# First block's weight sums of the output stages on VectorE, their stores three units later, last forms stored among the units, half of x reloaded later

## The chip, the cores and the metric

The kernel runs on one core of a Trainium2 chip. The metric is the device time of one execution in microseconds. Before the change three runs gave 2659.91 us (median; 2659.52 to 2662.99).

A core has five engines that run their own queues in order and wait for each other through semaphores: TensorE (PE, matrix products), VectorE (DVE), ScalarE (ACT), GpSimd (POOL) and SyncE (SP), whose queue here issues nearly all DMA transfers. Since each queue is in order, an instruction that waits holds back all that stand behind it on its engine.

## What is computed

Two layers of an encoder over 1024 positions of width 1024, float32. Layer 0 mixes by grouped-query attention, layer 1 by a chunked gMLP; each is followed by a squared-ReLU MLP of width 4096.

```python
for i in range(DEPTH):                                   # DEPTH = 2
    mod = cond @ ada_w[i] + ada_b[i]
    sh1, sc1, g1, sh2, sc2, g2 = jnp.split(mod, N_MOD, axis=-1)
    h = modulate(rmsnorm(x, norm1_g[i]), sh1, sc1)
    if i % N_MIXERS == 0:
        y = gqa_attention(...)
    else:
        y = chunked_gmlp(...)
    x = x + g1[:, None, :] * y
    h = modulate(rmsnorm(x, norm2_g[i]), sh2, sc2)
    x = x + g2[:, None, :] * sq_relu_mlp(h, mlp_w_in[i], mlp_w_out[i])

def chunked_gmlp(h, w_in, b_in, ln_g, ln_b, w_s, b_s, w_out):
    z = jax.nn.gelu(h @ w_in + b_in, approximate=False)
    u, v = jnp.split(z, 2, axis=-1)
    v = layernorm(v, ln_g, ln_b)
    ...                                                  # one 128x128 mix per group
    return (u * v) @ w_out                               # w_out: 3072 x 1024

def sq_relu_mlp(h, w_in, w_out):
    return jnp.square(jax.nn.relu(h @ w_in)) @ w_out     # w_out: 4096 x 1024
```

## The kernel before

Every large product is done by a seven-product scheme on 2 x 2 blocks (Winograd's form of Strassen's), and each product in three matmuls of a split float32: an operand becomes a high part (a cast on ScalarE) and a low part (source minus high part), and hi·hi, hi·lo and lo·hi are added up in PSUM. A *unit* is one product of 128 output rows by 512 positions over four 128-row slices: 12 matmuls of 128x512.

The three **output stages** are the second products of the two MLPs (`wm`) and of the gMLP (`wgo`), all by the class `Out`. It has 4 blocks of the inner dimension for an MLP and 3 for the gMLP. Its units run block by block in the order of the products 1, 2, 6, 7, 4, four units each (the pairs p = 0 to 3 of output rows), 20 units per block. Then, as a tail of 8 units per block, come the products 5 and 3 of all blocks, the last block first. Block 0 is units 0 to 19.

What a unit needs comes from two sides:

- The **weights**: the four blocks 11, 12, 21, 22 are loaded (`load_w`, `load_w2`). Products 6 and 7 need sums of them, made in `prep` (line 1134), three units ahead (`LO`). For product 6: 21 + 22 (line 1138), then that minus 11 (line 1140). For product 7: 12 − 11 (1142), then 22 − 11 (1144). The first sum of each kind is also the weight of product 5 or 3. It is needed only in the tail, and unless the block is the last one it is stored to DRAM by `keep` at once (line 1122) and loaded again by `load_kept` (line 1118). All four run on GpSimd (`G`). After the sum, `prep` casts the high half (line 1152, ScalarE) and subtracts for the low half (line 1153, VectorE), into a buffer of the tag `s`, of which there are five.
- The **forms**: seven combinations of the stage's input per 256 rows, in DRAM (`hidden`, `uv`; named hf). `load_f` loads one (line 1129), eight units ahead of its first unit; `split_f` splits it five units ahead (lines 318 and 319, ScalarE and VectorE).

The forms are written by the stage ahead. Three of a pair's seven are the results themselves (`early`); the other four come from `spread` (lines 1234 to 1237), which returns four store instructions that are put on a list `stores` and taken from it one by one. In the MLP `spread` runs on VectorE, in the gMLP on GpSimd, as do the gMLP's products u·v (`times`, line 1612). What is left on the list when the stage ahead ends is issued at once, before the output stage's first unit: at lines 1351 and 1352 in the MLP. In the gMLP, lines 1659 to 1661 first run the steps that are still due, for the last pair p = 11.

The residual x lies in 16 tiles, x[0] and x[1] for the two halves of the positions. Before the first MLP's and the gMLP's output stage it has been spilled to DRAM (xd), and is loaded again in four groups of four tiles, at the units that the table `XL` gives (line 1259). x[0] is added to from unit 4 on, x[1] only in the tail.

The program text isn't the order on the engines: a scheduler of the framework orders each engine's queue by its own estimate of when things are ready. So both the text and the resulting queues count.

Of the kernel before, what the change touches and what calls it, by code (L numbers as in the profile page):

```python
# [14 lines left out]
ALU = mybir.AluOpType  # L15
# [21 lines left out]
def encoder_kernel(ctx: ExitStack, tc: tile.TileContext, t: dict, out: bass.AP):  # L37
    nc = tc.nc
    V, S, G, T = nc.vector, nc.scalar, nc.gpsimd, nc.tensor
# [7 lines left out]
    def nm(s):  # L47
        uid[0] += 1
        return f"{s}_{uid[0]}"
# [825 lines left out]
    with ExitStack() as es:  # L875
# [132 lines left out]
        for i in range(nu + 2):  # L1008
# [7 lines left out]
            for op in ORDER.split():  # L1016
                f, w, j = op[0], int(op[1]), int(op[2])
# [39 lines left out]
    class Out:  # L1057
# [7 lines left out]
        def __init__(self, wsrc, forms, nblk, gate):  # L1065
            self.wsrc, self.forms, self.nblk, self.gate = wsrc, forms, nblk, gate
            self.n = 28 * nblk
            self.tail = 8 * nblk
            self.w, self.raw, self.f, self.sf, self.acc, self.ps = {}, {}, {}, {}, {}, {}
            last = nblk - 1  # L1070
            self.units = [(b, q, p) for b in range(nblk) for q in "12674" for p in range(4)]
            self.units += [(b, q, p) for q in "53" for b in (last, *range(last)) for p in range(4)]
            self.kept = {(b, q, p): dram.tile([P, 512], F32, name=nm("wf"))
                         for b in range(last) for q in "53" for p in range(4)}
            todo = []

            def at(i, fn, *args):
                todo.append((max(i, -OUT_PRE), len(todo), fn, args))

            for i, (b, q, p) in enumerate(self.units):  # L1080
                if q == "1":
                    at(i - LO - LW, self.load_w, b, "11", p)
                elif q == "2":
                    at(i - LO - (LW if b else LW2), self.load_w, b, "22", p)
                    if p % 2 == 0:
                        at(i - LO - LW, self.load_w2, b, "12", p // 2)
                        at(i - LO - (LW if b else LW2), self.load_w2, b, "21", p // 2)
                elif q in "53" and b < last:
                    at(i - LO - LK, self.load_kept, b, q, p)
            for i in range(0, self.n, 4):  # L1090
                for kt in range(4):
                    at(i + kt - FS - FA, self.load_f, self.units[i][:2] + (kt,))
            for i in range(0, self.n, 4):
                for kt in range(4):
                    at(i + kt - FS, self.split_f, self.units[i][:2] + (kt,))
            for i in range(self.n):
                at(i - LO, self.prep, i)
            self.todo = sorted(todo, key=lambda e: e[:2])

        def ahead(self, i):  # L1100
# [16 lines left out]
            self.w[k] = slot()  # L1117
            nc.sync.dma_start(self.w[k], self.kept[k])

        def keep(self, b, q, p, a):  # L1120
            if b < self.nblk - 1:
                nc.sync.dma_start(self.kept[(b, q, p)], a)
            else:
                self.w[(b, q, p)] = a

        def load_f(self, k):
            b, q, kt = k
# [6 lines left out]
        def prep(self, i):  # L1134
            b, q, p = self.units[i]
            a11, a12, a21, a22 = (self.w.get((b, c, p)) for c in ("11", "12", "21", "22"))
            if q == "6":
                G.tensor_tensor(a21, a21, a22, ALU.add)  # L1138
                self.keep(b, "5", p, self.w.pop((b, "21", p)))
                G.tensor_tensor(a11, a21, a11, ALU.subtract)  # L1140
            elif q == "7":
                G.tensor_tensor(a12, a12, a11, ALU.subtract)
                self.keep(b, "3", p, self.w.pop((b, "12", p)))
                G.tensor_tensor(a11, a22, a11, ALU.subtract)
                del self.w[(b, "11", p)]
            elif q == "4":
                del self.w[(b, "22", p)]
            src = self.w.pop((b, q, p)) if q in "53" else {"1": a11, "2": a12, "6": a11, "4": a22, "7": a11}[q]
            w_ = wide("s", F32R)
            hi, lo = w_[:, :512], w_[:, 512:]  # L1150
            self.sf[i] = hi, lo
            S.copy(hi, src)  # L1152
            V.tensor_tensor(lo, src, f32(hi), ALU.subtract)  # L1153
# [76 lines left out]
    def spread(tiles, dst, spare, eng):  # L1230

        b11, b12, b21, b22 = (tiles[a] for a in ((0, 0), (0, 1), (1, 0), (1, 1)))
        t3 = spare()
        eng.tensor_tensor(t3, b22, b12, ALU.subtract)
        eng.tensor_tensor(b12, b12, b11, ALU.subtract)
        eng.tensor_tensor(b11, b22, b12, ALU.subtract)
        eng.tensor_tensor(b21, b21, b11, ALU.subtract)
        return [lambda: nc.sync.dma_start(dst["7"], t3), lambda: nc.sync.dma_start(dst["5"], b12),
                lambda: nc.sync.dma_start(dst["6"], b11), lambda: nc.sync.dma_start(dst["4"], b21)]
# [16 lines left out]
            x[hf][k] = xslot()  # L1256
            nc.sync.dma_start(x[hf][k], xd[hf][k])

    XL = {-1: (0, 0), 2: (0, 1), 6: (1, 0), 10: (1, 1)}


    class Halves:
# [35 lines left out]
    def mlp(layer, fs, sqs, done, hook):  # L1298
# [4 lines left out]
        stores = []  # L1303
# [18 lines left out]
        n = 16 * 7  # L1322
# [25 lines left out]
            out_.ahead(i - n)  # L1348

        yield from winograd(lambda m: t["wi"][layer, m], 16, f, sink, FIRST, at, lambda: (cut(8), f.update(fs[0])))  # L1350
        while stores:
            stores.pop(0)()

        def at_out(i):
            if i == CUT:
                cut(4)
            if halves and i in XL:
                load_xs(*XL[i])
            if hook and i >= out_.n - out_.tail:
                hook(i - out_.n + out_.tail)  # L1360
# [58 lines left out]
    for ct in range(24):  # L1419
        i, r = divmod(ct, 3)  # L1420
# [129 lines left out]
    def gmlp(f, sqB, done, hook):  # L1550
# [26 lines left out]
        uv = forms_dram(12)  # L1577
        out_ = Out(t["wgo"], uv, 3, mod[:, 1, 2])
        us, vs, mixed, stores = {}, {}, {}, []
# [29 lines left out]

        def times(p, j, hf):  # L1610
            w_ = mixed[(2 * p + j, hf)]
            (G if (j, hf) in TG else V).tensor_tensor(w_, w_, us.pop((2 * p + j, hf)), ALU.mult)
            q = early((j, hf))
            if q:
                stores.append(lambda: nc.sync.dma_start(uv[p][q], w_))

        def spread_uv(p):
            tiles = {(j, hf): mixed.pop((2 * p + j, hf)) for j in range(2) for hf in range(2)}
            while stores:
                stores.pop(0)()  # L1620
            stores.extend(spread(tiles, uv[p], xslot, G))

        order = ((0, 0), (1, 0), (1, 1), (0, 1))
        steps = []
# [4 lines left out]
        for p in range(12):  # L1629
            i = 7 * p  # L1630
# [12 lines left out]
        def upto(i):  # L1643
            while steps and steps[0][0] <= i:
                _, _, fn, args = steps.pop(0)
                fn(*args)

        n = 12 * 7
# [7 lines left out]
        upto(-1)  # L1656
        for _ in winograd(lambda m: t["wu"][m], 12, f, sink, 0, at_u):
            pass
        upto(n + 9)
        while stores:  # L1660
            stores.pop(0)()
        load_xs(*XL[-1])

        def at_out(i):
            if i == CUT:
                cut(4)
            if i in XL:
                load_xs(*XL[i])
            if i >= out_.n - out_.tail:
                hook(i - out_.n + out_.tail)  # L1670
            if i == out_.n - PRE:
                next(mlp1)
# [27 lines left out]
FS = 5  # L1700
FA = 3
LO = 3
TG = ((0, 0), (1, 0), (1, 1), (0, 1))
CUT = 8
MX = 2
LW = 5
# [82 lines left out]
```

## Time and profile before

| | |
|---|---|
| median of 3 runs | 2659.91 us |
| the profiled execution | 2660.25 us |
| its span, first to last instruction | 2658.5 us |
| granted TensorE clock, mean | 0.996 |
| first MLP's output stage | from 962.31 us |
| gMLP's output stage | from 1794.32 us |
| second MLP's output stage | from 2345.95 us |

Times of instructions are microseconds from the start of the span. A row of the timeline gives start, duration, engine, line of the code, operation, output <- inputs, and in brackets how long the engine was idle before it and what ended that. A row of the waits gives who waited, for whom, the total, how many times and the longest. A row of the busy table gives a stretch and, for each engine, busy time and instructions in it, then the granted clock, the share of the DMA engines that was busy, and the rate that they moved. SPq is the SP queue. Names of tiles stand without numbers in the profile (t, s, w, c, x are the pools; out, mix are PSUM tiles).

### The profile page before, as it was taken

The numbers are of one execution on the slowest core, as the hardware profiler recorded it, in microseconds if no ns is written. First come the engines' busy times: TensorE is split into PE (matmuls) and PEld (weight loads), VectorE is DVE, ScalarE is ACT, GpSimd is POOL, SyncE is SP. The second block draws the span as 40 slices with busy tenths as digits, with TensorE's granted clock in tenths as the row PEclk, the third lists the DMA queues.
The fourth block names the chain that finished last, engine by engine and source line by source line (L and its number), as shares of the span: only waits on it lengthen the run. The fifth ranks groups of instructions, "written<-read, shape, count | busy, mean of one in ns | idle before, by whom it ended". The sixth has DMA issues, their size and how long they took to land.

```text
span 2658.5 us, 37214 instructions
## 1 busy us (share of the span) xinstructions
PE 2604.3 (98%) x12788; PEld 2166.5 (81%) x12788; DVE 2188.2 (82%) x3215; ACT 1451.1 (55%) x2616; POOL 819.4 (31%) x591
## 2 busy tenths in 40 slices
PE   7999999999999999999999999998999999999999
PEld 5788999887788878888788888887888788878887
DVE  7868999886999989977886687787978977789974
ACT  4569999945654455446543454444456655455442
POOL 0238776523000034430122054556520000035410
PEclk9999999999999999999999999999999999999999
DMA  8100222243486878644243355567741554478461
GB/s 286 42 33 7 74 88 74 96 128 126 173 289 237 285 268 305 201 135 174 72 135 109 121 181 172 179 210 283 240 135 52 174 174 157 153 278 284 151 209 61
DMA packets 208752, 435.38 MB, mean 164 GB/s; under 512 B 23025, under 2 KB 35441, under 8 KB 208562
## 3 DMA queue, kind: packets, MB, share of 16 engines
q1 hardware_dynamic: 181682, 395.24, 43.8%
q10 hardware_dynamic: 26880, 37.76, 3.9%
q8 instruction: 101, 1.65, 0.3%
q14 instruction: 89, 0.73, 0.1%
HBM read 310.23 MB, written 122.68 MB: 163 GB/s over the span
## 4 chain that ended last, share of the span: by engine, by line
PE 84%; DVE 7%; ACT 2%; DMA 2%; issue 2%; POOL 2%; SPq 0%; DVEq 0%; POOLq 0%; ACTq 0%
PE w L454 10%; PE w L455 10%; PE w L456 10%; PE out L1171 9%; PE out L1172 9%; PE out L1170 9%; PE s L907 4%; PE o L943 4%; PE t L924 4%; PE v L1517 3%; PE v L1518 3%; PE v L1516 3%; PE mix L1601 2%; DVE t L319 1%; PE qkv L559 1%
## 5 line engine op out<-in xcount | busy, mean ns | idle before, releaser
L1171 PE MATMUL out<-t,s 128*128 128x512 f32 x1232 | 481.8, 392 | 9.3 <-DVE t L319 9.2
L1170 PE MATMUL out<-t,s 128*128 128x512 f32 x1232 | 481.8, 392 | 4.0 <-ACT t L318 3.6
L1172 PE MATMUL out<-t,s 128*128 128x512 f32 x1232 | 479.6, 390 | 0.0
L454 PE MATMUL w<-t,s 128*128 128x512 f32 x1168 | 459.8, 395 | 0.0
L455 PE MATMUL w<-t,s 128*128 128x512 f32 x1168 | 454.8, 390 | 1.5 <-DVE t L319 1.5
L456 PE MATMUL w<-t,s 128*128 128x512 f32 x1168 | 454.6, 389 | 0.0
L319 DVE TENSOR_TENSOR t<-t,t 128x512 fp32r<-128x512 f32 x408 | 346.0, 860 | 39.9 <-ACT t L318 29.3
L318 ACT CAST t<-t 128x512 fp32r<-128x512 f32 x408 | 244.4, 616 | 121.9 <-DMA t<-hf 62.2
L1171 PEld LDWEIGHTS out<-t,s 128*128 128x128 f32 x1232 | 232.0, 188 | 63.1 <-DVE t L319 15.0
L1170 PEld LDWEIGHTS out<-t,s 128*128 128x128 f32 x1232 | 231.7, 188 | 55.8 <-ACT t L318 6.9
L1172 PEld LDWEIGHTS out<-t,s 128*128 128x128 f32 x1232 | 232.2, 188 | 47.7
L1138 POOL TENSOR_TENSOR w<-w,t 128x512 f32<-128x512 f32 x32 | 52.2, 1633 | 697.2 <-DMA t<-hf 613.2
L439 ACT CAST s<-w 128x512 fp32r<-128x512 f32 x292 | 174.0, 616 | 164.5 <-PE w L456 109.3
L455 PEld LDWEIGHTS w<-t,s 128*128 128x128 f32 x1168 | 219.4, 188 | 48.2 <-DVE t L319 3.5
L454 PEld LDWEIGHTS w<-t,s 128*128 128x128 f32 x1168 | 219.4, 188 | 48.2 <-issue 3.1
L1152 ACT CAST s<-t 128x512 fp32r<-128x512 f32 x240 | 148.0, 620 | 201.6 <-PE out L1172 143.0
L456 PEld LDWEIGHTS w<-t,s 128*128 128x128 f32 x1168 | 219.3, 188 | 45.4
L440 DVE TENSOR_TENSOR s<-w,s 128x512 fp32r<-128x512 f32 x292 | 220.6, 762 | 42.0 <-ACT s L439 41.4
L1153 DVE TENSOR_TENSOR s<-t,s 128x512 fp32r<-128x512 f32 x240 | 203.8, 850 | 60.7 <-ACT s L1152 59.9
L910 DVE TENSOR_REDUCE mx<-s 128x1 f32<-128x1024 f32 x128 | 156.2, 1220 | 32.8 <-PE s L907 31.5
L933 DVE TENSOR_TENSOR t<-t,t 128x512 fp32r<-128x512 f32 x256 | 164.1, 681 | 15.0 <-ACT t L927 14.2
L943 PE MATMUL o<-t,t 128*128 128x256 f32 x1024 | 162.6, 291 | 0.0
(242 smaller groups left out, 5128.4 us busy)
## 6 DMA issues: line engine op xcount, KB each, us to landing
t<-hf SPq DMA_DIRECT2D x320, 256.0 KB, 3.9
hf<-c SPq DMA_DIRECT2D x156, 256.0 KB, 2.6
w<-in_wi_dram SPq DMA_DIRECT2D x64, 512.0 KB, 4.2
hf<-c ACTq DMA_DIRECT2D x96, 256.0 KB, 2.4
w<-in_ada_dram SPq DMA_DIRECT2D x36, 512.0 KB, 3.6
x<-in_ada_dram SPq DMA_DIRECT2D x64, 256.0 KB, 6.0
t<-in_wm_dram SPq DMA_DIRECT2D x64, 256.0 KB, 5.2
wf<-w SPq DMA_DIRECT2D x64, 256.0 KB, 3.3
```

Source lines behind the costliest of these rows:

```text
L318: S.copy(hi, src)
L319: (eng or V).tensor_tensor(lo, src, f32(hi), ALU.subtract)
L439: S.copy(hi, src)
L440: V.tensor_tensor(lo, src, f32(hi), ALU.subtract)
L454: T.matmul(ps, hi[:, a], th, start=kt == 0, stop=False)
L455: T.matmul(ps, hi[:, a], tl, start=False, stop=False)
L456: T.matmul(ps, lo[:, a], th, start=False, stop=kt == 3)
L943: pin(T.matmul(u.po, vt[st][:, u.g * P : (u.g + 1) * P], src[:, s * 256 : (s + 1) * 256], start=st == 0 and part == 0, stop=st == 7 and pa ...
L1153: V.tensor_tensor(lo, src, f32(hi), ALU.subtract)
L1170: T.matmul(ps, hi[:, a], th, start=begin and kt == 0, stop=False, **g)
L1171: T.matmul(ps, hi[:, a], tl, start=False, stop=False, **g)
L1172: T.matmul(ps, lo[:, a], th, start=False, stop=end and kt == 3, **g)
```

## The change

In block 0 of each output stage the four weight sums of a pair are made on VectorE; the other blocks keep GpSimd. The stores of the first sums (for products 5 and 3) leave `prep` and become steps of their own, `KD` = 3 units after it, in all blocks but the last. What is left of `stores` at the end of the stage ahead is no longer issued in one go but one per unit of the output stage (from unit 3 on in the MLP). In the gMLP the steps due after the stage ahead's last unit, the last pair's products, `spread` and its stores, are taken along with the output stage's units, and for the last pair (p = 11) products and `spread` run on VectorE. The table `TG`, which had all products on GpSimd, goes. The two groups of x[1] are reloaded at units 20 and 30 instead of 6 and 10.

```diff
@@ class Out
             for i in range(self.n):
                 at(i - LO, self.prep, i)
+            for i, (b, q, p) in enumerate(self.units):
+                if q in "67" and b < last:
+                    at(i - LO + KD, self.store_kept, b, "5" if q == "6" else "3", p)
             self.todo = sorted(todo, key=lambda e: e[:2])
...
-        def keep(self, b, q, p, a):
-            if b < self.nblk - 1:
-                nc.sync.dma_start(self.kept[(b, q, p)], a)
-            else:
-                self.w[(b, q, p)] = a
+        def store_kept(self, *k):
+            nc.sync.dma_start(self.kept[k], self.w.pop(k))
...
             a11, a12, a21, a22 = (self.w.get((b, c, p)) for c in ("11", "12", "21", "22"))
+            e = G if b else V
             if q == "6":
-                G.tensor_tensor(a21, a21, a22, ALU.add)
-                self.keep(b, "5", p, self.w.pop((b, "21", p)))
-                G.tensor_tensor(a11, a21, a11, ALU.subtract)
+                e.tensor_tensor(a21, a21, a22, ALU.add)
+                self.w[(b, "5", p)] = self.w.pop((b, "21", p))
+                e.tensor_tensor(a11, a21, a11, ALU.subtract)
             elif q == "7":
-                G.tensor_tensor(a12, a12, a11, ALU.subtract)
-                self.keep(b, "3", p, self.w.pop((b, "12", p)))
-                G.tensor_tensor(a11, a22, a11, ALU.subtract)
+                e.tensor_tensor(a12, a12, a11, ALU.subtract)
+                self.w[(b, "3", p)] = self.w.pop((b, "12", p))
+                e.tensor_tensor(a11, a22, a11, ALU.subtract)
...
-    XL = {-1: (0, 0), 2: (0, 1), 6: (1, 0), 10: (1, 1)}
+    XL = {-1: (0, 0), 2: (0, 1), 20: (1, 0), 30: (1, 1)}
@@ mlp
-        while stores:
-            stores.pop(0)()
 
         def at_out(i):
+            if stores and i > 2:
+                stores.pop(0)()
@@ gmlp
-            (G if (j, hf) in TG else V).tensor_tensor(w_, w_, us.pop((2 * p + j, hf)), ALU.mult)
+            (V if p == 11 else G).tensor_tensor(w_, w_, us.pop((2 * p + j, hf)), ALU.mult)
...
-            stores.extend(spread(tiles, uv[p], xslot, G))
+            stores.extend(spread(tiles, uv[p], xslot, V if p == 11 else G))
...
-        upto(n + 9)
-        while stores:
-            stores.pop(0)()
         load_xs(*XL[-1])
 
         def at_out(i):
+            upto(n + i)
+            if stores:
+                stores.pop(0)()
...
-TG = ((0, 0), (1, 0), (1, 1), (0, 1))
+KD = 3
```

## The prediction, made before the result was known

> **What bounds the kernel now.** I read the page first, for the engine that sets the pace, then the busy table over chosen stretches, then the waits and the instructions in order of time inside them.
>
> ```profile
> span 2658.5 us, 37214 instructions
> PE 2604.3 (98%) x12788; PEld 2166.5 (81%) x12788; DVE 2188.2 (82%) x3215; ACT 1451.1 (55%) x2616; POOL 819.4 (31%) x591
> PE 84%; DVE 7%; ACT 2%; DMA 2%; issue 2%; POOL 2%; SPq 0%; DVEq 0%; POOLq 0%; ACTq 0%
> ```
>
> TensorE (PE) is busy 98% of the span and makes up 84% of the chain that ended last, and the change touches no matmul. So only PE's own holes can be won. The change touches the three output stages; unit 0 of each starts at 962.31, 1794.32 and 2345.95. The next table pairs the first ten units of each stage with an equally long stretch right after.
>
> ```profile
> core 0: us, PE busy (x) PEld busy (x) DVE busy (x) ACT busy (x) POOL busy (x), PEclk, DMA share, GB/s
> 962.30:995.00 32.70, 29.96 (x122) 23.26 (x121) 27.04 (x27) 16.14 (x30) 24.36 (x16) 0.95 0.68 235
> 995.00:1027.70 32.70, 32.70 (x146) 27.08 (x145) 27.36 (x34) 18.75 (x34) 13.61 (x9) 1.00 0.90 331
> 1794.30:1832.00 37.70, 30.75 (x122) 23.33 (x121) 22.66 (x20) 12.98 (x23) 30.92 (x22) 0.91 0.74 257
> 1832.00:1869.70 37.70, 37.70 (x167) 30.94 (x166) 34.23 (x41) 22.04 (x40) 19.12 (x12) 1.00 0.80 289
> 2345.90:2376.30 30.40, 28.08 (x122) 22.33 (x122) 27.08 (x27) 15.68 (x29) 23.09 (x15) 1.00 0.61 214
> 2376.30:2406.70 30.40, 30.37 (x134) 24.84 (x133) 25.31 (x34) 17.70 (x33) 9.45 (x7) 1.00 0.93 344
> ```
>
> Read the matmul counts, not the busy time: a slowed matmul counts as busy. The first stretch does 122 matmuls where the second does 146, 167 and 134. The lost time is 32.70 × (1 − 122/146) = **5.4 us** (first MLP), 37.70 × (1 − 122/167) = **10.2** (gMLP) and 30.40 × (1 − 122/134) = **2.7** (second MLP), 18.3 in all. That is the most that the named parts can return.
>
> ```profile
> 960.04 0.39 PE L456 MATMUL w<-t,s 128*128 128x512 f32 x1
> 962.31 0.39 PE L1170 MATMUL out<-t,s 128*128 128x512 f32 x1
> 962.76 0.39 PE L1172 MATMUL out<-t,s 128*128 128x512 f32 x1
> ...
> 990.14 0.80 PE L1171 MATMUL out<-t,s 128*128 128x512 f32 x1 [2.39 <-DVE t L319]
> ...
> 2345.95 0.39 PE L1170 MATMUL out<-t,s 128*128 128x512 f32 x1
> ```
>
> From 960.04 to 962.76 twelve matmuls pass, so a unit takes 2.72 us and a matmul 0.227. A hole costs its length, and the matmul after it takes 0.80 instead of 0.39. What PE lacks at 990.14 is the low half of a form (L319). Behind that:
>
> ```profile
> 979.33 0.62 ACT L318 CAST t<-t 128x512 fp32r<-128x512 f32 x1
> 984.85 0.62 ACT L1152 CAST s<-t 128x512 fp32r<-128x512 f32 x1 [4.89 <-POOL t L1140]
> ...
> SPq L1122 <- POOL w L1138: 8.4, 2, 4.5
> SPq L1122 <- POOL w L1138: 8.8, 3, 5.9
> SPq L1615 <- POOL c L1612: 4.0, 2, 2.7
> SPq L1122 <- POOL w L1138: 10.5, 3, 4.9
> ACT t L318 <- DMA t<-hf: 9.4, 2, 8.3
> ```
>
> ScalarE stands 4.89 us in front of a weight cast that needs a sum of GpSimd (POOL), and the form casts are queued behind it. The SP queue stands 8.4, 8.8 and 10.5 us (one row per stage, in order) before stores of such sums, with form loads behind them. In the gMLP stage the form casts also wait 9.4 us for their loads.
>
> **Weight sums to VectorE.** Per stage 16 sums leave POOL; in the gMLP stage 4 products and 4 subtractions of the last pair go too.
>
> ```profile
> L1138 POOL TENSOR_TENSOR w<-w,t 128x512 f32<-128x512 f32 x32 | 52.2, 1633 | 697.2 <-DMA t<-hf 613.2
> 968.62 1.77 DVE L1235 TENSOR_TENSOR c<-c,c 128x512 f32<-128x512 f32 x1
> 970.32 0.68 DVE L319 TENSOR_TENSOR t<-t,t 128x512 fp32r<-128x512 f32 x1
> 970.92 0.68 DVE L1236 TENSOR_TENSOR c<-c,c 128x512 f32<-128x512 f32 x1
> 971.52 0.68 DVE L1153 TENSOR_TENSOR s<-w,s 128x512 fp32r<-128x512 f32 x1
> 972.12 0.68 DVE L1237 TENSOR_TENSOR c<-c,c 128x512 f32<-128x512 f32 x1
> 972.73 0.68 DVE L1153 TENSOR_TENSOR s<-w,s 128x512 fp32r<-128x512 f32 x1
> ```
>
> On POOL 16 sums are 16 × 1.63 = 26 us, 6.5 per unit of 2.72: POOL is the late engine. On DVE with POOL quiet one starts 0.60 after another, so 16 are 9.6 us and 24 are 14.4. While POOL works, DVE instructions of the same shape take 1.77. In the first MLP stretch DVE is busy 27.04 for 27 instructions, 1.00 each; the same 27 at about 0.62 are 16.7, and with the sums 26.3 of the 27.2 that ten units need. So the work fits, barely, and order decides. The tightest place is the start of the second MLP's stage, where VectorE's queue splits the form of units 4 to 7 (t_23161 and on, four tiles); L1153 there is the low half of a weight. Before:
>
> ```order
> L319 TENSOR_TENSOR t_23176<-t_23091,t_23175 128x512
> L1153 TENSOR_TENSOR s_23307<-t_23010,s_23307 128x512
> L319 TENSOR_TENSOR t_23204<-t_23124,t_23203 128x512
> L319 TENSOR_TENSOR t_23230<-t_23158,t_23229 128x512
> L319 TENSOR_TENSOR t_23254<-t_23173,t_23253 128x512
> ```
>
> and with the change (L1139 and L1141 are the sums, L1154 the former L1153):
>
> ```order
> L319 TENSOR_TENSOR t_23172<-t_23091,t_23171 128x512
> L1154 TENSOR_TENSOR s_23253<-w_23122,s_23253 128x512
> L1139 TENSOR_TENSOR w_23156<-w_23156,t_23154 128x512
> L1154 TENSOR_TENSOR s_23278<-w_23122,s_23278 128x512
> L319 TENSOR_TENSOR t_23200<-t_23124,t_23199 128x512
> L1141 TENSOR_TENSOR t_23010<-w_23156,t_23010 128x512
> L1139 TENSOR_TENSOR w_23156<-w_23156,t_23167 128x512
> L1139 TENSOR_TENSOR w_23195<-w_23195,t_23193 128x512
> L1154 TENSOR_TENSOR s_23304<-t_23010,s_23304 128x512
> L319 TENSOR_TENSOR t_23226<-t_23158,t_23225 128x512
> ```
>
> Four sums now stand among the last splits. The fourth tile's split is the 17th instruction from L1234:
>
> ```profile
> 965.21 1.78 DVE L1234 TENSOR_TENSOR t<-c,c 128x512 f32<-128x512 f32 x1
> 2348.20 0.98 DVE L1234 TENSOR_TENSOR t<-c,c 128x512 f32<-128x512 f32 x1 [1.36 <-ACT c L1307]
> ```
>
> That is 2348.20 + 16 × 0.60 = 2357.8; casts that wait for a free weight buffer (five in turn, so unit 7's waits for the end of unit 2, 2345.95 + 3 × 2.72 = 2354.1) move it to about 2358.4, done at 2359.1. PE wants it 58 matmuls into the stage: 2345.95 + 58 × 0.227 = 2359.1. On time or a few tenths late: I leave **0.3** of the 2.7. By the same count the first MLP's is due at 975.5 and done near 975.8; with one slow matmul I leave **0.8** of 5.4.
>
> The Trainium skill, page "VectorE: DVE Perf Modes", section "The DRAIN you can't avoid", says that the next instruction does not start until the pipe is empty, that is, after the whole duration. By it the pitch would be 0.68 and not 0.60. The rows above, 0.60 apart at 0.68 long, speak against it here; its price stands among the rivals.
>
> **Stores three units later, last forms among the units.** Nothing is added, only positions change. The SP queue at the start of the first MLP's output stage (hf: stored forms; wf: stored sums). Before:
>
> ```order
> L1238 DMA hf_7868<-t_10803 128x512
> L1238 DMA hf_7866<-c_10719 128x512
> L1239 DMA hf_7867<-c_10658 128x512
> L1107 DMA t_10833<-in_wm_dram 128x512
> L1239 DMA hf_7865<-c_10639 128x512
> L1129 DMA t_10835<-hf_7762 128x512
> L1107 DMA t_10859<-in_wm_dram 128x512
> L1129 DMA t_10863<-hf_7769 128x512
> L1122 DMA wf_7869<-w_10810 128x512
> ```
>
> After:
>
> ```order
> L1239 DMA hf_7868<-t_10803 128x512
> L1110 DMA t_10829<-in_wm_dram 128x512
> L1129 DMA t_10831<-hf_7762 128x512
> L1239 DMA hf_7866<-c_10719 128x512
> L1110 DMA t_10855<-in_wm_dram 128x512
> L1129 DMA t_10859<-hf_7769 128x512
> L1240 DMA hf_7867<-c_10658 128x512
> L1110 DMA t_10883<-in_wm_dram 128x512
> L1129 DMA t_10885<-hf_7776 128x512
> L1240 DMA hf_7865<-c_10639 128x512
> L1129 DMA t_10917<-hf_7783 128x512
> L1124 DMA wf_7869<-w_10810 128x512
> ```
>
> Loads of weights and of the next form no longer wait for four stores, and the sum's store comes behind all four form loads. The delayed forms belong to the last pair, first read in the last block, 40 units or more later in every stage: free. A late store holds its weight buffer 3 × 2.72 = 8.2 us longer; the last leaves at unit 15, and the next block's sums begin at unit 25, 27 us on:
>
> ```profile
> w<-in_wm_dram SPq DMA_DIRECT2D x24, 512.0 KB, 5.9
> ```
>
> A 5.9 us load fits; without that cover it would cost up to its 5.9 once per block.
>
> **Half of x later.** In the first MLP the 16 reloads stand at the same places of the SP queue as before: nothing. In the gMLP stage eight move behind the first block's form loads: 8 × 256 KB at the 257 GB/s of that stretch is 8.2 us of transfer out of the way. Their tiles are first added after unit 60, so nobody waits.
>
> **The gMLP stage** has the largest term. VectorE's queue there, around the last PSUM adds of the stage ahead (L473, L476). Before:
>
> ```order
> L1153 TENSOR_TENSOR s_18189<-t_18008,s_18189 128x512
> L1605 SCALAR_TENSOR_TENSOR c_18108<-mix_18103,cols,x_17572 128x512
> L319 TENSOR_TENSOR t_18186<-t_18083,t_18185 128x512
> L319 TENSOR_TENSOR t_18216<-t_18111,t_18215 128x512
> L473 TENSOR_TENSOR c_17970<-w_4096_18120,c_17970 128x512
> ```
>
> After:
>
> ```order
> L1154 TENSOR_TENSOR s_18189<-t_18008,s_18189 128x512
> L1139 TENSOR_TENSOR w_18181<-w_18181,t_18179 128x512
> L1141 TENSOR_TENSOR t_18004<-w_18181,t_18004 128x512
> L473 TENSOR_TENSOR c_17970<-w_4096_18120,c_17970 128x512
> L476 TENSOR_TENSOR c_18135<-w_4096_18120,c_18070 128x512
> ```
>
> The sum L1139 waits for a weight, t_18179, and DVE's whole queue stands behind it. Its load and the sum on POOL were:
>
> ```profile
> 1786.42 0.44 SPq L1107 DMA_DIRECT2D t<-in_wgo_dram  x1
> 1790.97 0.68 DVE L473 TENSOR_TENSOR c<-w,c 128x512 f32<-128x512 f32 x1
> 1792.90 1.76 POOL L1138 TENSOR_TENSOR w<-w,t 128x512 f32<-128x512 f32 x1 [7.93 <-DVE c L1605]
> ```
>
> If it lands at 1792.9 again, L473 moves from 1790.97 to about 1794.2. Some 19 instructions later stands the last split for unit 4: about 1794.2 + 19 × 0.61 = 1805.8, done 1806.5; due 1794.3 + 57 × 0.227 = 1807.2. That is 0.7 us to spare; a load 2 us later costs 1.3. I leave **1.0** of 10.2.
>
> **Sum.** 18.3 − 0.8 − 1.0 − 0.3 = 16.2. The profiled execution took 2660.25 us (span 2658.5 and 1.75 around it), 0.34 above the median of 2659.91. Forecast 2660.25 − 16.2 = **2644.0**.
>
> **Rivals.** (1) *VectorE has no overlap or SP is later than I count*: 16, 16 and 21 instructions ahead of the three dead lines at 0.68 each instead of 0.60 are 1.3, 1.3 and 1.7 us more, 4.3 in all: 2648.3. For it: the margins above are under 1 us. The skill's section gives this same case. (2) *The waits move over*: what POOL waited for, DVE now waits for.
>
> ```profile
> POOL w L1138 <- DMA t<-in_wm_dram: 5.3, 1, 5.3
> POOL w L1138 <- DMA t<-in_wgo_dram: 6.1, 1, 6.1
> POOL w L1138 <- DMA t<-in_wm_dram: 4.6, 1, 4.6
> ```
>
> All paid on PE, 16.0 of the 18.3 come back: 2658, no change. Against it: the weights are now issued ahead of the stores, which is why they were late. (3) *VectorE becomes the bound, slower*: if its instructions stay at 1.00 us each (POOL quiet or not), the added work is no longer hidden. The stretches leave it idle 5.7 + 15.0 + 3.3 = 24.0 us, against 56 × 0.60 = 33.6 added; 9.6 of overflow and the 16.0 of waits, less 18.3, give +7.3: 2667.6. It decides from 27.2 / 43 = 0.63 us per instruction on; the 0.60 rows are just below. (4) *The change doesn't do what it says*: true of x in the first MLP, already priced at nothing.
>
> **Numbers.** My case 0.64 (2641 to 2647), rival 1 0.17 (to 2654), rival 2 0.12, rival 3 0.07. A measurement of this kernel tells about 0.2%, 5.3 us, from no change: faster 0.81, same 0.12, slower 0.07. The range runs from all 18.3 and a little of later holes, 2640.5, to the end of rival 1, 2653.5; that leaves out rivals 2 and 3, 0.19.
>
> **What would show it.** Right: 140 matmuls or so in the first 32.7 us of each output stage, POOL idle there, DVE rows near 0.68 long, no SP wait for POOL in block 0, ScalarE no longer waiting for L1140. Wrong: PE waiting for L319 at unit 4 or 8 with DVE busy without a gap (rival 1 or 3), or DVE idle before L1139 for a DMA with PE idle behind it (rival 2).

## The result, and the profile after

The changed kernel takes **2642.2 us** (median of 4 runs, 2639.86 to 2649.06) against 2661.1 us of the kernel before, run on the same chip (4 runs, 2659.52 to 2662.99). The ratio is 0.9936, with a 95% interval of 0.9923 to 0.9949: 0.64% faster. The forecast was 2644.0 us in a range of 2640.5 to 2653.5. The profiled execution after took 2640.55 us, 19.7 less than the 2660.25 before.

The head of the page, after. PE has the same 12788 matmuls and is busy 7.0 us less, since slowed matmuls count as busy. VectorE has 56 instructions more and is yet busy 4.9 us less in all. That is the first sign that the added work isn't paid for at its own price:

```profile
span 2638.8 us, 37172 instructions
PE 2597.3 (98%) x12788; PEld 2165.1 (82%) x12788; DVE 2183.3 (83%) x3271; ACT 1451.1 (55%) x2616; POOL 729.8 (28%) x535
```

The busy table after, over the first ten units or so of each output stage, the same lengths as the first, third and fifth rows before:

```profile
core 0: us, PE busy (x) PEld busy (x) DVE busy (x) ACT busy (x) POOL busy (x), PEclk, DMA share, GB/s
961.60:994.30 32.70, 32.70 (x146) 27.03 (x145) 30.34 (x49) 18.63 (x35) 0.00 (x0) 1.00 0.84 303
1787.60:1825.30 37.70, 37.70 (x168) 31.23 (x167) 36.02 (x59) 20.83 (x38) 0.00 (x0) 1.00 0.89 310
2330.10:2360.50 30.40, 30.40 (x136) 24.96 (x135) 28.20 (x47) 17.53 (x33) 0.00 (x0) 1.00 0.90 313
```

PE does 146, 168 and 136 matmuls where it did 122 three times. GpSimd does nothing. VectorE puts 49, 59 and 47 instructions through in the time in which it did 27, 20 and 27. Its busy time is about 0.61 us per instruction (a row of the timeline lasts 0.68 and overlaps the next by 0.08), where it was 1.00 or more.

Where the 19.7 us come from is read from the stages' starts after (timeline of PE, the first matmul of unit 0):

```profile
961.58 0.39 PE L1171 MATMUL out<-t,s 128*128 128x512 f32 x1
1787.59 0.39 PE L1171 MATMUL out<-t,s 128*128 128x512 f32 x1
2330.18 0.39 PE L1171 MATMUL out<-t,s 128*128 128x512 f32 x1
```

| from | to | before, us | after, us | difference | predicted |
|---|---|---|---|---|---|
| start of the span | first MLP's output stage | 962.31 | 961.58 | −0.7 | 0 |
| first MLP's output stage | gMLP's output stage | 832.01 | 826.01 | −6.0 | −4.6 |
| gMLP's output stage | second MLP's output stage | 551.63 | 542.59 | −9.0 | −9.2 |
| second MLP's output stage | end of the span | 312.55 | 308.62 | −3.9 | −2.4 |

The gMLP's row holds a loss that is new. At the stage's second block GpSimd makes four sums, as before, and now they fall beside form splits that are due. Three rows of the timeline after, of GpSimd, VectorE and PE:

```profile
1882.29 7.08 POOL L1139 TENSOR_TENSOR c<-c,t 128x512 f32<-128x512 f32 x4 [12.70 <-DMA t<-in_wgo_dram]
1884.76 1.78 DVE L1154 TENSOR_TENSOR s<-t,s 128x512 fp32r<-128x512 f32 x1
1888.98 0.47 PE L1171 MATMUL out<-t,s 128*128 128x512 f32 x1 [0.59 <-ACT t L318]
```

VectorE's instruction takes 1.78 us beside them, and 4 us later PE stands. With a like hole at 1892, counted from start to start, it is 1.4 us. The experiments below come back to what this loss needs.

### The profile page after: what moved, and what is told of

It reads as the page before. It is cut to its first block, busy times and chain, and to the rows that moved or that the text cites. A ratio compares the mean times of both kernels' runs of the same rounds, so it can differ in the third digit from the quotient of the medians.

```text
span 2638.8 us, 37172 instructions
## 1 busy us (share of the span) xinstructions
PE 2597.3 (98%) x12788; PEld 2165.1 (82%) x12788; DVE 2183.3 (83%) x3271; ACT 1451.1 (55%) x2616; POOL 729.8 (28%) x535
## 5 line engine op out<-in xcount | busy, mean ns | idle before, releaser
L319 DVE TENSOR_TENSOR t<-t,t 128x512 fp32r<-128x512 f32 x408 | 329.5, 818 | 32.7 <-ACT t L318 22.4
L1139 POOL TENSOR_TENSOR w<-w,t 128x512 f32<-128x512 f32 x20 | 32.4, 1622 | 775.7 <-DMA t<-hf 415.6
L1154 DVE TENSOR_TENSOR s<-t,s 128x512 fp32r<-128x512 f32 x240 | 193.7, 808 | 59.1 <-ACT s L1153 58.4
L933 DVE TENSOR_TENSOR t<-t,t 128x512 fp32r<-128x512 f32 x256 | 164.2, 682 | 15.9 <-ACT t L927 15.1
```

The costliest lines, as they stand in the source:

```text
L319: (eng or V).tensor_tensor(lo, src, f32(hi), ALU.subtract)
L933: pin(V.tensor_tensor(lo, pt, f32(hi), ALU.subtract))
```

## The experiments

Two theories stood against each other at first. **Engine**: GpSimd's sums in block 0 were the cause, by being late, by slowing VectorE, or both. **Queue**: the order on SP was the cause, since loads stood behind stores that waited. First each part of the change was made alone on the kernel before, then single parts of the change were undone, then GpSimd and VectorE were loaded on purpose.

In the busy tables below each row is the first 54.4 us of an output stage, the time of block 0's 20 units. A row with no hole has 240 to 242 matmuls, and each that is missing is 0.227 us. For comparison, the kernel before:

```profile
962.30:1016.70 54.40, 51.66 (x217) 41.23 (x216) 43.41 (x50) 28.66 (x53) 27.28 (x17) 0.97 0.80 288
1794.30:1848.70 54.40, 47.45 (x194) 36.88 (x193) 37.09 (x40) 23.82 (x43) 34.31 (x23) 0.94 0.83 299
2345.90:2400.30 54.40, 52.05 (x226) 41.86 (x226) 46.68 (x55) 30.12 (x55) 26.30 (x17) 1.00 0.79 290
```

and the changed kernel:

```profile
961.60:1016.00 54.40, 54.40 (x241) 45.00 (x240) 46.77 (x71) 31.45 (x58) 5.45 (x4) 1.00 0.86 307
1787.60:1842.00 54.40, 54.40 (x242) 45.05 (x241) 47.39 (x73) 29.79 (x54) 4.57 (x3) 1.00 0.88 304
2330.20:2384.60 54.40, 54.40 (x241) 44.87 (x240) 47.91 (x72) 32.11 (x58) 8.12 (x6) 1.00 0.93 323
```

### One part at a time on the kernel before

**The sums alone.** In `prep`:

```diff
+            e = G if b else V
-                G.tensor_tensor(a21, a21, a22, ALU.add)
+                e.tensor_tensor(a21, a21, a22, ALU.add)
...
```

> The kernel before, with only block 0's weight sums on VectorE; their stores stay right behind the sums, the other three parts as before. Lost time in the first ten units of the three output stages before: 5.4, 10.2 and 2.7 us by the matmul counts. If the holes come from GpSimd's sums (my theory): 1 us or less is lost in the two MLP stages and about 5 in the gMLP stage, where GpSimd's last products and subtractions still stand ahead: about 2648 us. If they come from the SP queue standing before stores (rival): the stores still wait, now for VectorE, and less than 3 us comes back: 2657 or more.

Measured: 2654.51 us, ratio 0.9979 (0.9969 to 0.9988). Busy table of this run, the three stages:

```profile
958.90:1013.30 54.40, 54.40 (x241) 44.99 (x241) 46.76 (x71) 31.73 (x58) 6.03 (x5) 1.00 0.88 311
1786.90:1841.30 54.40, 46.42 (x195) 37.43 (x194) 42.70 (x57) 23.92 (x45) 10.76 (x7) 0.91 0.78 282
2338.50:2392.90 54.40, 54.40 (x241) 44.69 (x240) 47.35 (x70) 32.11 (x58) 6.66 (x5) 1.00 0.89 310
```

The ten executions spread from 2648.95 to 2658.52 us, and the profiled one, which these rows show, is the fastest. Of its 11.3 us, 3.4 are won ahead of the first output stage, which starts at 958.95, 4.1 and 3.8 from the two MLP stages on to the next mark, and 0.1 in the gMLP stage. The median lies between the two expectations. The MLP stages do what the first one says; the gMLP stage, for which it has about 5 us of loss, loses 10.6.

In the profiled execution both MLP stages are free of holes by this part alone, although the SP queue still has its four stores ahead of the loads. The gMLP stage is as bad as before, 195 against 194. Why, the timeline of this run tells (GpSimd, SP, VectorE and PE):

```profile
1797.27 1.63 POOL L1237 TENSOR_TENSOR c<-c,c 128x512 f32<-128x512 f32 x1
1802.46 0.38 SPq L1107 DMA_DIRECT2D t<-in_wgo_dram  x1
1807.01 0.69 DVE L1139 TENSOR_TENSOR w<-w,t 128x512 f32<-128x512 f32 x1 [5.29 <-DMA t<-in_wgo_dram]
1808.96 0.80 PE L1172 MATMUL out<-t,s 128*128 128x512 f32 x1 [5.73 <-DVE t L319]
```

GpSimd is still at the last pair's `spread` (L1235 to L1238) 10 us into the stage. SP stands in front of the stores of these forms, and a weight load is issued only at 1802.46. The sum, now in VectorE's queue, waits 5.29 us for it with a form split queued behind, and PE waits 5.73. That is the prediction's rival 2, waits that move to VectorE, and in this kernel it is what happens. With the rest of the change the stage has no hole in block 0.

**The late stores alone** (`store_kept` three units after `prep`, sums on GpSimd):

```diff
-                nc.sync.dma_start(self.kept[(b, q, p)], a)
+                at(i - LO + KD, self.store_kept, b, "5" if q == "6" else "3", p)
...
```

> The kernel before, with only the stores of the first sums moved three units later; the sums stay on GpSimd. If GpSimd's sums are the cause: under 2 us comes back, 2658 or more, and ScalarE still stands before the weight cast for a sum. If the SP queue's standing is the cause: half of the 18.3 us or more comes back, 2651 or less.

Measured: 2658.66 us, ratio 0.9998 (0.9989 to 1.0007): nothing. SP waits of this run in the first MLP stage:

```profile
SPq L1124 <- POOL w L1139: 7.8, 2, 4.2
```

**The last steps among the units alone:**

```diff
-        while stores:
-            stores.pop(0)()
 
         def at_out(i):
+            if stores and i > 2:
+                stores.pop(0)()
...
```

(in the gMLP `upto(n + i)` in `at_out` for `upto(n + 9)` ahead of it).

> The kernel before, with only the left-over form stores (and in the gMLP the last pair's steps) taken along with the output stage's units; every sum, product and subtraction stays on the engine it had. If GpSimd's sums are the cause: the MLP stages keep most of their loss, 3 us or more and 1.5 or more, and 2 to 5 us come back in all: 2655 to 2658. If the SP queue's standing is the cause: 9 us or more, 2651 or less.

Measured: 2662.51 us, ratio 1.0010 (1.0001 to 1.0020): a little slower. The gMLP stage gains, 215 matmuls where it had 194. Both MLP stages lose, 201 and 204 where they had 217 and 226. Busy table of the first 13.7 us of the first MLP stage, of the kernel before and of this one:

```profile
962.30:976.00 13.70, 13.70 (x60) 10.85 (x59) 11.77 (x14) 8.36 (x16) 5.83 (x4) 1.00 0.58 201
```

```profile
961.10:974.80 13.70, 11.98 (x53) 9.57 (x52) 12.07 (x10) 9.36 (x19) 10.47 (x7) 1.00 0.70 249
```

Weights arrive earlier once the stores don't stand ahead of them (249 GB/s against 201), GpSimd makes 7 sums here and not 4, and VectorE, beside it, gets through 10 instructions and not 14. So earlier loads made things worse in the MLP stages as long as GpSimd made the sums. The queue theory has the sign wrong there and right in the gMLP stage. The engine theory's 2655 to 2658 us missed too: it had no price for loads that come earlier.

**Late x alone:**

```diff
-    XL = {-1: (0, 0), 2: (0, 1), 6: (1, 0), 10: (1, 1)}
+    XL = {-1: (0, 0), 2: (0, 1), 20: (1, 0), 30: (1, 1)}
```

> The kernel before, with only x[1] reloaded at units 20 and 30 instead of 6 and 10. If GpSimd's sums are the cause: only the gMLP stage can change, by 1 to 2 us: 2658 to 2659. If the gMLP's 10.2 us are form loads queued behind the reload (rival): half of them or more comes back, 2655 or less. The two MLP stages stay as they were under both.

Measured: 2659.88 us, ratio 1.0001 (0.9991 to 1.0010): nothing.

### One part of the change undone

**Sums back on GpSimd:**

```diff
-            e = G if b else V
+            e = G
```

> The changed kernel with block 0's weight sums back on GpSimd; late stores, late forms, late x and the last pair's products and spread on VectorE stay. Engine theory (GpSimd is the late engine in block 0: 1.63 us or more per sum, and VectorE beside it at 1.77): the holes of both MLP output stages come back, 5 to 9 us each, and those of the gMLP stage in part, since its four sums per pair stand on GpSimd again: ratio to before 0.998 to 1.001, 2655 to 2662 us. Queue theory (the order of loads and stores on SP is what counts, and all of it stays): 2640 to 2646 us, no holes in the first ten units.

Measured: 2659.78 us, ratio to before 1.0007 (0.9998 to 1.0016). All that was won is gone. The MLP stages have 207 and 205 matmuls in their first 54.4 us, and the gMLP stage this row of the busy table:

```profile
1796.70:1851.10 54.40, 51.77 (x227) 42.21 (x226) 49.81 (x55) 28.22 (x51) 29.51 (x20) 1.00 0.89 329
```

Of the gMLP's loss about two thirds stay away without the sums: 227, where it had 194 before. The expected sign was right for all stages.

**Late stores and late x undone together:**

```diff
-KD = 3
+KD = 0
-    XL = {-1: (0, 0), 2: (0, 1), 20: (1, 0), 30: (1, 1)}
+    XL = {-1: (0, 0), 2: (0, 1), 6: (1, 0), 10: (1, 1)}
```

> The changed kernel with the sums' stores issued at once after the sum again (KD = 0) and x[1] reloaded at units 6 and 10 again; sums and last pair on VectorE and the last steps among the units stay. If these two parts do nothing, as each alone did: first ten units of all three stages free of holes, 2640 to 2645 us, within 0.1% of the changed kernel. If the stores' place matters once VectorE makes the sums: SP stands before stores behind which form loads are queued, 1 to 4 us of holes per stage come back, 2645 to 2652 us.

Measured: 2642.46 us, ratio 0.9929 (0.9917 to 0.9942), the same as the changed kernel. All three stages have 241 or 242 matmuls. In the time of the whole kernel these two parts are worth nothing, alone or beside the others.

One place differs. At the gMLP stage's second block this run has no hole, 122 matmuls in 27.2 us (the changed kernel has 115 there, its row stands at the last experiment). GpSimd's four sums slow VectorE there just as much. The busy table and VectorE's timeline, of this run:

```profile
1870.60:1897.80 27.20, 27.20 (x122) 22.52 (x121) 24.68 (x35) 13.09 (x23) 8.61 (x5) 1.00 0.88 321
```

```profile
1887.31 1.78 DVE L1154 TENSOR_TENSOR s<-t,s 128x512 fp32r<-128x512 f32 x1
```

So GpSimd's sums alone don't make the new 1.4 us of the changed kernel. The next two runs, which keep the late stores and the late x, have no hole there either (121 matmuls each). What else the loss needs was not tested.

In the first MLP stage SP stands just as long as with the late stores (SP waits of this run and of the changed kernel, in turn):

```profile
SPq L1124 <- DVE w L1143: 11.3, 4, 6.1
```

```profile
SPq L1124 <- DVE w L1143: 10.4, 3, 6.9
```

Here a queue that stands 10 us in front of a store cost nothing. The likely reason, not tested by itself, is that what is queued behind the store was wanted later still.

**The last steps ahead of the units again** (sums and last pair stay on VectorE):

```diff
+        upto(n + 9)
+        while stores:
+            stores.pop(0)()
...
-            upto(n + i)
-            if stores:
-                stores.pop(0)()
```

> The changed kernel with the left-over form stores issued at once again ahead of the output stage, and in the gMLP the steps of the last pair all taken before it; sums on VectorE, late stores, late x, last pair on VectorE stay. Engine theory: the MLP stages stay free of holes (the sums alone freed them), the gMLP stage too, because its last pair no longer needs GpSimd: 2640 to 2645 us. Queue theory for the gMLP stage (four stores and the last steps ahead of the first units block SP and VectorE): 6 to 10 us of its 10.4 come back, 2648 to 2653 us, with the MLP stages free.

Measured: 2644.85 us, ratio 0.9944 (0.9928 to 0.9961). The MLP stages stay free (241 each). The gMLP stage loses 4.6 us again, less than the queue theory's 6 to 10. The time lies in the engine theory's 2640 to 2645, but that theory had the gMLP stage free of holes, so neither was right.

**The gMLP's last pair back on GpSimd:**

```diff
-            (V if p == 11 else G).tensor_tensor(w_, w_, us.pop((2 * p + j, hf)), ALU.mult)
+            G.tensor_tensor(w_, w_, us.pop((2 * p + j, hf)), ALU.mult)
...
-            stores.extend(spread(tiles, uv[p], xslot, V if p == 11 else G))
+            stores.extend(spread(tiles, uv[p], xslot, G))
```

> The changed kernel with the gMLP's last pair (4 products, 4 subtractions of its spread) back on GpSimd; all else stays, the left-over steps among the units too. If the place of the gMLP's loss was GpSimd's backlog from that last pair: 4 to 10 us back in the gMLP stage alone, 2646 to 2652 us. If it was only that these steps and their stores stood ahead of the stage's first units: gMLP stage below 2 us of loss, 2640 to 2645 us. The MLP stages are not touched by it: 0 in both cases.

Measured: 2645.49 us, ratio 0.9951 (0.9936 to 0.9966). The gMLP stage loses 2.6 us, between the two expectations. Its rows, with the last steps ahead and with the last pair on GpSimd, in turn:

```profile
1789.70:1844.10 54.40, 51.87 (x221) 42.00 (x220) 46.39 (x73) 28.86 (x53) 4.04 (x3) 0.97 0.83 294
```

```profile
1792.30:1846.70 54.40, 52.11 (x230) 42.84 (x229) 48.48 (x64) 28.13 (x51) 17.31 (x12) 1.00 0.89 320
```

So the gMLP stage needs three of the parts: the sums on VectorE, the last steps among the units and the last pair on VectorE. Any one missing leaves 227, 221 or 230 matmuls, and only all three together give 242.

### Loading the engines on purpose

**GpSimd busy, nobody waiting.** To the changed kernel, in `prep`, work is added whose result is never read; the order of the instructions of VectorE, ScalarE, PE and SP, as the trace names them, is that of the changed kernel:

```diff
+            if b == 0 and q in "67":
+                for _ in range(8):
+                    G.tensor_tensor(scr, a22[:, :P], ones, ALU.add)
```

> The changed kernel with added work on GpSimd that nobody reads: in block 0 eight additions of 128x128 at each preparation of a product 6 or 7 (64 per stage), into a scratch tile; the order on the other engines does not change. Theory of the shared access (VectorE is slow while GpSimd works, 1.77 against 0.68 us per instruction): VectorE's instructions in the first ten units go up to 0.8 us or more on the mean, its 43 to 59 instructions no longer fit, and holes come back although nobody waits for GpSimd: 2 to 6 us per stage, 2646 to 2658 us in all. Theory of the wait (only waiting for GpSimd's results cost time): VectorE may slow down, PE stays free of holes: 2640 to 2644 us.

Measured: 2669.75 us, ratio to before 1.0040 (1.0025 to 1.0055): slower than the kernel before. Busy table of this run:

```profile
965.60:1020.00 54.40, 50.99 (x212) 40.25 (x211) 52.77 (x63) 27.83 (x53) 47.34 (x62) 0.97 0.74 254
1801.30:1855.70 54.40, 49.06 (x205) 39.15 (x204) 52.97 (x65) 25.20 (x46) 44.82 (x59) 0.97 0.74 254
2351.60:2406.00 54.40, 49.41 (x205) 38.88 (x204) 52.87 (x63) 27.11 (x50) 47.70 (x63) 0.97 0.75 260
```

No row of the waits in these stretches has anyone waiting for GpSimd. Yet some 100 matmuls are missing, 23 us. VectorE gets through 63 to 65 instructions where 71 to 73 were due. The timeline of this run, GpSimd and VectorE:

```profile
971.56 9.46 POOL L1141 TENSOR_TENSOR scr<-t,ones 128x128 f32<-128x128 f32 x11
...
971.96 0.95 DVE L1241 TENSOR_TENSOR c<-c,c 128x512 f32<-128x512 f32 x1
972.83 0.95 DVE L1158 TENSOR_TENSOR s<-w,s 128x512 fp32r<-128x512 f32 x1
```

GpSimd's additions stand 9.46 / 11 = 0.86 us apart, and VectorE's instructions 0.87. So the two engines' instructions go in turn here, one for one, and a VectorE instruction that needs 0.60 alone takes as long as GpSimd's does. PE's holes end, as in the kernel before, with the low half of a form (a row of the waits, first MLP stage):

```profile
PE out L1176 <- DVE t L320: 2.6, 2, 1.8
```

**Half the dose** (`range(4)` for `range(8)`):

> The run with GpSimd busy at half the dose: four unread additions of 128x128 on GpSimd at each preparation in block 0, 32 per stage at 0.76 us, 24 us per stage: about the GpSimd time that the kernel before spent there on its 16 sums (26 us), but nobody waits for it. The full dose lost 24.5 us in the three stages. If the loss is in proportion to GpSimd's time: about 12 us, 2652 to 2656 us, and GpSimd's mere work explains most of the kernel before's loss. If VectorE has some slack that the half dose uses up without a hole (an addition at 0.76 us costs VectorE about 0.22, so 7 us per stage, of some 6 to 9 to spare): 0 to 4 us, 2642 to 2647 us, and then the loss before needed the wait for GpSimd's results or its larger additions (1.63 us, VectorE at 1.77) on top.

Measured: 2655.47 us, ratio to before 0.9983 (0.9974 to 0.9993). Block 0 of the three stages:

```profile
960.80:1015.20 54.40, 52.60 (x231) 42.95 (x230) 49.99 (x70) 29.57 (x56) 23.72 (x32) 1.00 0.82 284
1792.80:1847.20 54.40, 53.70 (x236) 43.83 (x235) 50.08 (x72) 27.71 (x50) 20.86 (x29) 1.00 0.81 286
2340.50:2394.90 54.40, 51.62 (x220) 41.95 (x219) 48.76 (x68) 28.74 (x54) 25.34 (x33) 0.97 0.82 284
```

Against the changed kernel half the dose costs about 13 us (2655.47 − 2642.2) and the full dose about 28. That is about in proportion (in block 0 alone, 37 missing matmuls against some 100); the expectation of slack that hides half of it missed. With 24 us of GpSimd per stage, about as much as the 16 sums took, some 70% of the 18.9 us between the kernels are gone, although nothing waits for GpSimd.

The sum hides that the places differ. In block 0 some 10, 6 and 21 matmuls are missing where the kernel before misses 24, 48 and 15, and the rest of the loss lies outside block 0. So at this dose a slowed VectorE gives more than all of the second MLP's holes, under half of the first MLP's, and an eighth of the gMLP's.

**The same additions on VectorE** (`V.tensor_tensor` in the same place):

> The same eight unread additions of 128x128 at each preparation in block 0 as in the run with GpSimd busy, but made by VectorE itself; GpSimd stays idle. An addition of this size should take about 0.2 us of VectorE, 64 per stage 13 us. If the loss in the run with GpSimd busy (2669.75 us, 24.5 us more in the three stages than the changed kernel) came through VectorE's time alone, taking that time directly must open holes of the same kind, 2 to 5 us in the first ten units of each stage and 4 to 9 us in the whole stage: 2655 to 2670 us. If VectorE has room for it (below 2 us per stage): 2642 to 2648 us, and then GpSimd's work cost by another way than VectorE's time.

Measured: 2661.44 us, ratio to before 1.0002 (0.9992 to 1.0011). The time is as expected, the place isn't: no hole in the first ten units, all from unit 12 on, about 7 us for each stage as a whole. The timeline of this run shows what one addition takes from VectorE:

```profile
970.23 0.28 DVE L1141 TENSOR_TENSOR scr<-t,ones 128x128 f32<-128x128 f32 x1
970.43 0.68 DVE L1143 TENSOR_TENSOR w<-w,t 128x512 f32<-128x512 f32 x1
```

It is 0.20 us from start to start, so 64 are 13 us per stage, and about half of that reaches PE. VectorE is idle for 7.6, 7.0 and 6.5 us of the 54.4 us in the changed kernel. GpSimd doing these additions costs more (about 28 us) than VectorE doing them itself (about 19 us). The two prices are not of the additions alone, since in this run the scheduler also put the queues of VectorE, ScalarE and SP partly in another order.

**All sums on VectorE**, which follows from this:

```diff
-            e = G if b else V
+            e = V
```

> The changed kernel with the weight sums of all blocks on VectorE, not block 0's alone. If GpSimd's work costs VectorE more time than the sum itself takes there (1.5 us of GpSimd hold VectorE's instructions at 1.77 or 0.9 us; a sum on VectorE takes 0.60): VectorE gets freer in blocks 1 to 3, the two holes of the gMLP stage at its second block (1.4 us) go, 2638 to 2641 us. If VectorE has no room there beside the PSUM adds: new holes, 2 to 6 us per stage, 2646 to 2658 us. Within 0.1% of the changed kernel if neither.

Measured: 2641.53 us, ratio 0.9924 (0.9910 to 0.9938). It can't be told from the changed kernel in time, but the new holes are gone, as expected (as they are in the last three runs of the section before, which keep GpSimd's sums there). Busy table around them, of this run and of the changed kernel:

```profile
1867.30:1894.50 27.20, 27.20 (x122) 22.52 (x121) 26.96 (x45) 12.48 (x22) 0.00 (x0) 1.00 0.78 268
```

```profile
1866.30:1893.50 27.20, 26.12 (x115) 21.02 (x114) 24.00 (x34) 14.31 (x25) 9.68 (x6) 1.00 0.86 318
```

VectorE does 45 instructions in the time in which it did 34. This version beats the kernel before and is not behind the changed one.

## Why the prediction was right

**Right: where the time was.** The three stages' first ten units, and PE's holes in them. The bound of 18.3 us was a little low. Counted from start to start the first ten units lost 5.4, 10.4 and 3.1 us, and the second MLP's stage as a whole got 3.9 us shorter.

**Right: the main part.** The sums on VectorE carry both MLP stages (sums alone: 241 matmuls each; all but the sums: 207 and 205). The signs named for it were there: GpSimd idle, VectorE near 0.6 us, ScalarE no longer waiting for GpSimd. But ScalarE still waits, 7.6 us in all, now for VectorE's sums, where it waited 8.0 for GpSimd's, and PE does not. The waits in the first MLP stage, before and then after:

```profile
ACT s L1152 <- POOL t L1140: 8.0, 2, 4.9
```

```profile
ACT s L1153 <- DVE t L1141: 4.9, 2, 2.6
ACT s L1153 <- DVE t L1145: 2.7, 3, 1.4
```

So the 4.89 us of ScalarE that the prediction quoted were by themselves no proof of a loss. PE waited for the splits of forms (L319), and the runs with GpSimd busy show that a slowed VectorE is enough to make these late.

**Right: the tightest place.** The prediction named the splits of the second MLP's form of units 4 to 7, wanted 58 matmuls into the stage, and left 0.3 us for them. There PE's weight load waited 0.3 us for such a split (a row of the waits after), and PE lost 0.1 us some 60 matmuls in:

```profile
PEld out L1172 <- DVE t L319: 0.3, 1, 0.3
```

**Mis-sized: what is left.** The prediction left 0.8, 1.0 and 0.3 us of holes in the first ten units; 0.0, 0.0 and 0.1 were left. In the gMLP stage the order of the queue was as foreseen: the sum L1139 stands before the PSUM add L473 and waits for its weight, and L473 waits behind it. The step that failed is when the weight lands. On the chip (timeline after, SP and VectorE):

```profile
1778.82 0.42 SPq L1110 DMA_DIRECT2D t<-in_wgo_dram  x1
...
1784.29 0.69 DVE L1139 TENSOR_TENSOR w<-w,t 128x512 f32<-128x512 f32 x1 [1.38 <-DMA t<-in_wgo_dram]
...
1785.62 0.68 DVE L473 TENSOR_TENSOR c<-w,c 128x512 f32<-128x512 f32 x1
```

The load goes out at 1778.82, where before it was 1786.42, and the sum starts 3.3 us ahead of unit 0, which is at 1787.59. The prediction had let the weight land at 1792.9, 1.4 us ahead of unit 0, as before. So VectorE stood for 1.38 us before the sum, but L473 ran 2.0 us ahead of unit 0 and not 0.1, and PE lost nothing by it. With 1.0 left over and nothing set aside for the new 1.4 us at the second block, the gMLP's term came out right (9.2 and 9.0) by two errors of opposite sign. That part of the hit is luck.

**A slip in the working.** The 6.5 us of GpSimd are four sums, a pair's, and not a unit's: a unit of product 6 or 7 needs two, 3.3 us. That is still more than a unit's 2.72, so GpSimd is late, but by less than the prediction says.

**Wrong in its reason: SP.** The prediction counted the SP queue's waits of 8 to 10 us among the causes, with the late stores as their cure. In the MLP stages that is refuted: the stores' place and that of x change nothing in either direction, and SP stands as long after. In the gMLP stage the timeline of the sums alone has SP in front of the last pair's stores (L1239, L1240), not in front of those of the sums; that this wait was the cause there is read from the order of events, no run undoes it alone. There the loss needed three parts to go, which the prediction's one term for the stage did not tell apart.

**The rivals.** Rival 1 (VectorE without overlap) fell: its instructions start 0.60 apart with GpSimd quiet. The section of the Trainium skill that the prediction cites for it, page "VectorE: DVE Perf Modes", section "The DRAIN you can't avoid", adds that a next instruction that isn't held starts earlier. The rows of this case, 0.60 apart at 0.68 long, agree with that sentence. Rival 2 (waits move to VectorE) is real in the kernel with the sums alone, 5.29 us in the gMLP stage; in the changed kernel 1.38 us of it are left, which cost PE nothing. Rival 3 (VectorE becomes the bound) was rightly placed near: 13 us more per stage on VectorE, 39 in all, gave about 19 us back. Its price for the change itself was wrong, as it held VectorE's slow instructions against the added work, when the same move takes the slowness away.

What isn't settled is how the kernel before's loss splits between waiting for GpSimd and being slowed by it. The half dose took quarter-size additions, spread otherwise than the real sums, and its losses lie in other stages than those of the kernel before.

## What to carry to other kernels

When GpSimd and VectorE work side by side, price a GpSimd instruction by what it takes from VectorE too: 1.1 us here for a 128x512 addition (VectorE's start-to-start goes from 0.60 to 1.70), more than the 0.60 that VectorE needs to do it itself. That price holds for VectorE instructions that read both inputs from SBUF, the memory of the tiles, and none from PSUM. A stretch where VectorE is nearly full is the place to keep GpSimd quiet. And before a queue's wait is believed to be a cause, undo it alone: here 10 us of it cost nothing.

## What the runs showed of the hardware

VectorE's and GpSimd's additions took turns, one for one: VectorE's started 0.87 us apart beside 128x128 additions (GpSimd's 0.86), 1.70 beside 128x512 ones, against 0.60 alone. I had expected VectorE to be slower by a share, not to be locked to the other's step. The Trainium skill, page "SBUF — State Buffer", section "Who interferes with whom", says that a VectorE instruction with two SBUF inputs contends with a GpSimd instruction that reads SBUF, and that the pair of ports that the two engines share is an exclusive lock. The rows agree, and the busy runs give its price. They also show the other side: of VectorE's instructions beside GpSimd's four sums (1882.29 to 1889.37, timeline after) those that take one input from PSUM (out) were not slowed, 0.68 us where L1154 took 1.78:

```profile
1883.05 0.68 DVE L1223 TENSOR_TENSOR t<-out,t 128x512 f32<-128x512 f32 x1
...
1888.16 0.68 DVE L1223 TENSOR_TENSOR t<-out,t 128x512 f32<-128x512 f32 x1
```

The first matmul after a hole took 0.47 us after 0.59 us of idling, 0.80 after 2.39 and after 5.73. The prediction's 0.80 after every hole was too simple, and its one slow matmul too few. In the kernel before, after the hole of 2.39 us, the next six also took 0.60 to 0.63 us, 0.43 from start to start where 0.227 is the rule (the first two, timeline before):

```profile
990.74 0.63 PE L1172 MATMUL out<-t,s 128*128 128x512 f32 x1
991.17 0.63 PE L1170 MATMUL out<-t,s 128*128 128x512 f32 x1
```

So that hole cost 1.6 us more than its length, and the granted clock of its stretch was 0.95. As no such hole was left, the forecast was not hurt by it.
